# Four chunks of seven block products in each feed-forward, with weights relaid in 4 KB rows

## The chip, the cores and the metric

The kernel runs on one core of a Trainium2 chip. The metric is the device time of one execution in microseconds (us). Engines of the core work side by side, each in the order of its own instruction stream: TensorE (PE, with its weight loads shown as PEld), VectorE (DVE), ScalarE (ACT), GpSimd (POOL) and SyncE (SP), which issues the transfers between device memory and the on-chip buffer.

## What is computed

A block of two layers on 256 tokens of width 1024, in fp32. Six stages follow each other, each ending in a residual sum and a layer normalization: a gated feed-forward, a hybrid mixer (a gated delta rule beside a state-space scan), a feed-forward, a feed-forward, an attention mixer (NSA), a feed-forward. A feed-forward is

```
def swiglu(x, w_in, w_out):
    gate, up = jnp.split(x @ w_in, 2, axis=-1)
    return (jax.nn.silu(gate) * up) @ w_out
```

with `w_in` of 1024 x 5632 and `w_out` of 2816 x 1024. After each stage comes `layer_norm(x * alpha + 0.5 * y)` for a feed-forward, without the 0.5 for a mixer.

## The kernel before

**Precision.** A product of fp32 numbers is made of three faster products. Each operand is split into a high part (rounded to the type fp32r) and a low part (the rest), and the kernel adds high x high, high x low and low x high. `split` (L646) does it: a copy that rounds, on ACT or DVE (on ACT alone while `self.hard` is set, as in a feed-forward), and a subtraction, always on DVE. Weights are split on the chip too: a raw tile arrives by transfer, then `whi` and `wlo` are made of it (`unit`, L655). One such pair of 128 x 1024 costs one ACT and one DVE instruction.

**Feed-forward** (`ffn`, L1046). The 2816 inner columns are 22 tiles of 128, 11 steps of 256. The first two steps (NT) are done with the tokens as the stationary operand (`proj_tok`), then come ordinary steps with the weights stationary (`proj_two`, L867: eight matmuls of 512 columns and eight of 256 for each tile of 128 columns), each followed by gating on ACT and DVE. Four steps' worth of columns go another way: two *chunks* of 512 columns (`wide`, L745). There the 256 tokens and the 1024 inputs are cut in halves, gate and up weights are the two halves of the columns, and the 2 x 2 block product is made of seven block products in place of eight (in the manner of Strassen and Winograd), from sums and differences of blocks. The weight sums are made on DVE, 8 additions of 128 x 1024 a chunk (`add`), then split; the token sums once per stage (`token_forms`, L728). A product is twelve matmuls of 512 columns. The result has tokens on partitions and is transposed by eight 128 x 128 transposes. `WIDE` (L51) says in which half-steps the chunks' parts are issued between the ordinary ones.

**Output.** Each of the 22 inner tiles is one term of the second product: twelve matmuls into four accumulators (`out_mm`, L1063). The last few terms of the second token block are held back (`LAG`, 5) until the first block's normalization has begun.

**Order.** The program is first written down as a list; `Plan.order` (L344) then simulates the engines with a cost for each instruction and writes down a fixed order for each engine's stream. Buffers are 36 tiles of 128 x 1024 (`m4`) with quotas by purpose, four raw tiles of 128 x 2048 and two tiles for x. A load is issued by SP when its raw tile is free. POOL does little in a feed-forward but one power for each normalization (`lnve`).

All instructions have line L546 in the profile, since they are issued there; they are told apart by tile names.

Of the kernel before, what the change touches and what calls it, by code (L numbers as in the profile page):

```python
# [18 lines left out]
P = 128  # L19
# [7 lines left out]
RAW, M4 = 4, 36  # L27

CAPS = {
    "raw": (RAW, "SB"), "m4": (M4, "SB"), "x": (2, "SB"),  # L30
# [4 lines left out]
QUOTAS = {"M": None, "D": None, "F": None, "S": (8, 8), "Z": (4, 4), "L": (4, 4), "G": (6, 6), "P": (5, 5), "Q": (5, 5), "W": (12, 24)}  # L35

KEPT = ("L", "G", "F")
# [13 lines left out]
WIDE = ("", "ab", "cd", "ef", "g", "ab", "cd", "ef", "g", "")  # L51
# [4 lines left out]
KEEP_WARM = 5500  # L56

# [121 lines left out]
class Plan:  # L179
# [81 lines left out]
    def price(self, op, eng, fn, args, kw):  # L261
# [15 lines left out]
        if fn == "dma_start":  # L277
            return 60.0
# [65 lines left out]
    def order(self, caps):  # L344
# [25 lines left out]
        dma_free = 0.0  # L370
# [69 lines left out]
        while left:  # L440
# [58 lines left out]
            if fn == "dma_start":  # L499

                dma_free = max(dma_free, st + 1300) + op.nbytes / (290.0 if st < 8000.0 else 360.0)
                op.end = dma_free + 600
                free[e] = st + c
            else:
                op.end = st + c
                free[e] = st + c
# [63 lines left out]
class K:  # L570
    NT = 2
    LAG = 5
# [82 lines left out]
    def unit(self, srcs, parts):  # L655

        raw = self.plan.tile("raw", [P, 2048], F32, "raw", stream="W")
        for dst, src in srcs:
            self.nc.sync.dma_start(dst(raw), src)
        out = []  # L660
        for f in parts:
            v = f(raw)
            n = int(v.ids.size)
            shape = v.shape
            hi = self.m4(n, "whi", "W", F32R)
            lo = self.m4(n, "wlo", "W", F32R)
            if len(shape) == 3:
                hi, lo = (t.rearrange("p (a b) -> p a b", a=shape[1]) for t in (hi, lo))
            self.split(hi, lo, v)
            out.append((hi, lo))  # L670
        return out

    def unit_cols(self, w, c0, n):

        v3 = lambda r: r[:, :KD * n].rearrange("p (k n) -> p k n", k=KD)
        parts = [lambda r, e=e: v3(r)[:, :, e * P:(e + 1) * P] for e in range(n // P)]
        return self.unit([(v3, w[:, :, c0:c0 + n])], parts)

    def unit_rows(self, w, k0, nk, c0, n):

        v3 = lambda r: r[:, :nk * n].rearrange("p (k n) -> p k n", k=nk)
        g = min(nk, 1024 // n)
        out = self.unit([(v3, w[:, k0:k0 + nk, c0:c0 + n])],
                        [lambda r, e=e: v3(r)[:, e:e + g, :] for e in range(0, nk, g)])
        return [(hi[:, k, :], lo[:, k, :]) for hi, lo in out for k in range(g)]

    def tok_weights(self, w, c0, n):

        nk = 2048 // n
        out = []  # L690
        for k0 in range(0, KD, nk):
            out += self.unit_rows(w, k0, min(nk, KD), c0, n)
        return out

    def pair_weights(self, w, c0, c1, n):

        out = []
        for k0 in range(0, KD, 4):
            raw = self.plan.tile("raw", [P, 2048], F32, "raw", stream="W")
            for g, c in enumerate((c0, c1)):  # L700
                dst = raw[:, g * 1024:g * 1024 + 4 * n]
                self.nc.sync.dma_start(dst.rearrange("p (k n) -> p k n", k=4), w[:, k0:k0 + 4, c:c + n])
            v = raw.rearrange("p (g k n) -> p k g n", g=2, k=4)
            for e in range(0, 4, 2):
                hi, lo = self.m4(1024, "whi", "W", F32R), self.m4(1024, "wlo", "W", F32R)
                self.split(*(t.rearrange("p (k g n) -> p k g n", k=2, g=2) for t in (hi, lo)), v[:, e:e + 2])
                hi, lo = (t.rearrange("p (k c) -> p k c", k=2) for t in (hi, lo))
                out += [(hi[:, k, :], lo[:, k, :]) for k in range(2)]
        return out

    def first_weights(self, w, c0, arrivals):

        out = []
        for k0 in range(0, KD, 2):
            if k0 % 4 == 0:
                raw = self.plan.tile("raw", [P, 2048], F32, "raw", stream="W")
            v = H3(raw[:, k0 % 4 * 512:(k0 % 4 + 2) * 512], 2)
            hi, lo = (H3(self.m4(1024, n, "W", F32R), 2) for n in ("whi", "wlo"))
            step = 1 if arrivals and k0 < 4 else 2
            for e in range(0, 2, step):  # L720
                self.nc.sync.dma_start(v[:, e:e + step], w[:, k0 + e:k0 + e + step, c0:c0 + 512])
                self.split(hi[:, e:e + step], lo[:, e:e + step], v[:, e:e + step])
                for f in (arrivals.pop(0) if arrivals else []):
                    f()
            out += [(hi[:, k, :], lo[:, k, :]) for k in range(2)]
        return out

    def token_forms(self, x):  # L728

        V = self.nc.vector  # L730
        (a11, a21), (a12, a22) = ((X[:, 0], X[:, 1]) for X in x[3])
# [5 lines left out]
        for X in x[3]:  # L737
            hi, lo = (self.m4(1024, n, "F", F32R).rearrange("p (b k t) -> p b k t", b=2, k=4) for n in ("fhi", "flo"))
            self.split(*(t.rearrange("p b k t -> p (b k t)") for t in (hi, lo, X)))
            out += [(hi[:, b], lo[:, b]) for b in range(2)]  # L740
        s2, s3, s4, s1 = out
        part = lambda b, k0: tuple(x[e][:, k0:k0 + 4, b, :] for e in range(2))
        return dict(a=part(0, 0), b=s1, c=part(0, 4), d=s2, e=s3, f=part(1, 4), g=s4)

    def wide(self, w_in, c0, forms, gout, then):  # L745

        nc, V = self.nc, self.nc.vector
        h4 = lambda t: H3(t, 4)

        def load(k0, c):  # L750
            raw = self.plan.tile("raw", [P, 2048], F32, "raw", stream="W")
            nc.sync.dma_start(h4(raw), w_in[:, k0:k0 + 4, c:c + 512])
            return raw

        def halves(src):
            out = []
            for e in range(2):
                hi, lo = self.m4(1024, "whi", "W", F32R), self.m4(1024, "wlo", "W", F32R)
                self.split(hi, lo, src[:, e * 1024:e * 1024 + 1024])
                out.append((H3(hi, 2), H3(lo, 2)))  # L760
            return out

        def add(out, a, b):
            for e in range(2):
                cs = slice(e * 1024, e * 1024 + 1024)
                V.tensor_tensor(out[:, cs], a[:, cs], b[:, cs], OP.add)

        def product(bank, name, w, start):
            ah, al = forms[name]

            def mm(*args, start=False, stop=False, on={} if start else dict(skip_group_check=True)):
                nc.tensor.matmul(*args, start=start, stop=stop, **on)
            for e, (wh, wl) in enumerate(w):
                for k in range(2):
                    n = 2 * e + k
                    mm(bank, ah[:, n], wh[:, k], start=start and n == 0)
                    mm(bank, al[:, n], wh[:, k])
                for k in range(2):
                    n = 2 * e + k
                    mm(bank, ah[:, n], wl[:, k], stop=n == 3)  # L780

        b11 = load(0, c0)
        w = halves(b11)
        b12 = load(0, DFF + c0)
        p, q = self.bank("mp"), self.bank("mp")
        s, u, v, sg = (H3(self.m4(1024, n, "F"), 2)[:, e] for n in ("su", "vg") for e in range(2))
        product(p, "a", w, True)
        nc.scalar.activation(s, p, AF.Copy)
        yield
        add(b11, b11, b12)  # L790
        product(q, "b", halves(b11), True)
        yield
        b21 = load(4, c0)
        product(p, "c", halves(b21), False)
        nc.scalar.activation(sg, p, AF.Silu)
        yield
        b22 = load(4, DFF + c0)
        add(b11, b11, b22)
        product(p, "d", halves(b11), True)
        V.tensor_tensor(u, p, s, OP.add)  # L800
        yield
        add(b12, b12, b22)
        product(p, "e", halves(b12), False)
        V.tensor_tensor(v, p, s, OP.add)
        V.tensor_tensor(v, q, v, OP.subtract)
        yield
        add(b11, b11, b21)
        product(p, "f", halves(b11), False)
        V.tensor_tensor(s, p, s, OP.add)
        nc.scalar.activation(s, s, AF.Silu)  # L810
        yield
        product(q, "g", halves(b22), False)
        V.tensor_tensor(u, q, u, OP.subtract)
        V.tensor_tensor(sg, sg, u, OP.mult)
        V.tensor_tensor(s, s, v, OP.mult)
        gh, gl = gout
        for b, g in enumerate((sg, s)):
# [3 lines left out]
            self.split(gh[:, :, b * P:(b + 1) * P], gl[:, :, b * P:(b + 1) * P], h4(pt))  # L821
        then()
# [10 lines left out]
    def new_x(self, name="x"):  # L833

        t = self.plan.tile("x", [P, KD, 2, 2, P], F32R, "x", stream="")
        return [t[:, :, 0], t[:, :, 1], t]

    def new_forms(self, x):

        x.append([self.m4(1024, f"X{q}", "F").rearrange("p (b k t) -> p b k t", b=2, k=4) for q in range(2)])  # L840
        return x

    def transpose_half(self, x, b, h, q, scale=None, c0=None):
# [7 lines left out]
        if len(x) > 3:  # L851
# [1381 lines left out]
```

## Time and profile before

| | before |
|---|---|
| median of 3 runs | 1104.2 us (1102.8 to 1106.8) |
| the profiled execution | 1103.9 us |
| its span (first to last instruction) | 1102.2 us |
| PE / DVE / ACT / POOL busy | 1082.8 / 939.7 / 653.3 / 45.1 us |
| moved by DMA | 201 MB |
| packets under 2 KB / under 8 KB | 90074 / 132314 |

Busy time is the time in which an engine had an instruction in flight. Matmuls overlap and their ends are modelled, so PE at 98% need not be PE at its peak; the starts of the weight loads tell more. In names, `whi` and `wlo` are the weights' parts, `raw` the weights as they arrive, `x` the tokens' parts, `fhi` and `flo` the parts of the token sums, `g`, `gh`, `gl` the gated tiles, `ps`, `mp`, `acc` accumulators. `su` and `vg` hold a chunk's intermediate results, `sg` an ordinary step's.

### The profile page before, as it was taken

What the parts mean: (1) busy time and instruction counts of PE and PEld (TensorE: products, weight loads), DVE (VectorE), ACT (ScalarE), POOL (GpSimd) and SP (SyncE); (2) the same over time, 40 slices, a digit from 0 to 9 for tenths busy, and PEclk for the clock granted to TensorE, in tenths of its full rate; (3) what the DMA queues carried; (4) which work ended last, traced back from release to release, by engine and by line L of the source; (5) the groups of instructions that cost most, each with busy time, mean ns of one, the idle gap of its engine ahead of it and who ended that gap; (6) DMA issues with size and microseconds to landing.
All of it is one profiled execution on the core that took longest, in us unless ns stands there. A gap on an engine that the chain in (4) does not pass through costs nothing.

```text
span 1102.2 us, 16098 instructions
## 1 busy us (share of the span) xinstructions
PE 1082.8 (98%) x6234; PEld 917.0 (83%) x6234; DVE 939.7 (85%) x1417; ACT 653.3 (59%) x1106; POOL 45.1 (4%) x85
## 2 busy tenths in 40 slices
PE   9999999998999999999999999999999999999997
PEld 6888878897999887888888888888887778888885
DVE  7969879798969999969877988979778979879694
ACT  7647565168736756647464756647356777556460
POOL 1000000002000311000000000000000100000000
PEclk9999999999999999999999999999999999999999
DMA  9628468542825175539369445639526227446361
GB/s 309 236 104 295 147 221 280 191 137 65 243 93 204 68 251 180 202 115 314 106 238 296 162 145 194 209 127 301 181 84 255 77 80 267 151 169 217 118 222 39
DMA packets 132391, 201.01 MB, mean 182 GB/s; under 512 B 9485, under 2 KB 90074, under 8 KB 132314
## 3 DMA queue, kind: packets, MB, share of 16 engines
q1 hardware_dynamic: 132314, 199.97, 53.6%
q8 instruction: 49, 0.80, 0.3%
q14 instruction: 28, 0.23, 0.1%
HBM read 197.18 MB, written 1.07 MB: 180 GB/s over the span
## 4 chain that ended last, share of the span: by engine, by line
PE 57%; DVE 3%; ACT 1%; issue 0%; DVEq 0%
PE ps L546 25%; PE acc L546 19%; PE mp L546 14%; DVE arena L546 1%; DVE h L546 1%; ACT whi L546 1%; DVE wlo L546 0%; DVE P L546 0%; DVE qs L546 0%; DVE x L546 0%; DVE whi L546 0%; DVE vbd L546 0%; DVE lnst L546 0%; DVE kd L546 0%; DVE qT L546 0%
## 5 line engine op out<-in xcount | busy, mean ns | idle before, releaser
L546 DVE TENSOR_TENSOR wlo<-raw,whi 128x1024 fp32r<-128x1024 f32 (+2 forms) x399 | 473.1, 1208 | 58.5 <-ACT whi L546 57.1
L546 ACT ACTIVATE whi<-raw 128x1024 fp32r<-128x1024 f32 (+2 forms) x374 | 374.5, 1045 | 96.0 <-DMA raw<-in_ffn_w_in_dram 47.7
L546 PE MATMUL ps<-x,whi 128*128 128x512 f32 (+2 forms) x1072 | 247.4, 352 | 2.6 <-ACT cv L546 2.2
L546 PEld LDWEIGHTS ps<-x,whi 128*128 128x128 f32 (+1 forms) x1072 | 185.4, 189 | 28.1 <-ACT cv L546 3.5
L546 PE MATMUL ps<-x,wlo 128*128 128x256 f32 x856 | 153.2, 284 | 0.0
L546 PE MATMUL acc<-whi,g 128*128 128x512 f32 x444 | 145.8, 390 | 0.0
L546 PEld LDWEIGHTS ps<-x,wlo 128*128 128x128 f32 x856 | 129.1, 190 | 6.5
L546 PE MATMUL ps<-whi,x 128*128 128x512 f32 (+1 forms) x480 | 129.4, 386 | 0.9 <-ACT x L546 0.5
L546 PEld LDWEIGHTS ps<-whi,x 128*128 128x128 f32 x480 | 85.7, 188 | 17.0 <-issue 1.1
L546 PEld LDWEIGHTS acc<-whi,g 128*128 128x128 f32 x444 | 83.5, 188 | 16.7
L546 PE MATMUL acc<-wlo,g 128*128 128x512 f32 x222 | 86.9, 391 | 0.0
L546 ACT ACTIVATE sg<-ps 128x256 f32<-128x256 f32 x92 | 34.8, 379 | 70.3 <-PE ps L546 69.8
L546 DVE TENSOR_TENSOR raw<-raw,raw 128x1024 f32<-128x1024 f32 x64 | 75.8, 1217 | 0.3
L546 PE MATMUL acc<-whi,x 128*128 128x512 f32 x224 | 73.8, 404 | 1.9 <-DVE x L546 1.0
L546 PE MATMUL ps<-wlo,x 128*128 128x512 f32 (+1 forms) x240 | 68.1, 382 | 0.0
L546 DVE TENSOR_TENSOR sg<-ps,sg 128x256 f32<-128x256 f32 (+1 forms) x94 | 39.7, 424 | 17.2 <-ACT sg L546 15.9
L546 PE MATMUL mp<-whi,x 128*128 128x512 f32 x192 | 51.5, 390 | 1.0 <-DVE vg L546 0.6
L546 PE MATMUL mp<-whi,fhi 128*128 128x512 f32 x128 | 50.3, 393 | 0.8 <-ACT whi L546 0.5
L546 PEld LDWEIGHTS acc<-whi,x 128*128 128x128 f32 x224 | 41.4, 188 | 11.1 <-ACT whi L546 2.1
L546 PE MATMUL mp<-whi,flo 128*128 128x512 f32 x128 | 49.9, 390 | 0.0
L546 PE MATMUL acc<-whi,gh 128*128 128x512 f32 x127 | 49.7, 391 | 0.0
L546 PE MATMUL acc<-wlo,gh 128*128 128x512 f32 x127 | 49.7, 391 | 0.0
(287 smaller groups left out, 1575.7 us busy)
## 6 DMA issues: line engine op xcount, KB each, us to landing
raw<-in_ffn_w_in_dram SPq DMA_DIRECT2D x72, 1024.0 KB, 5.2
raw<-in_ffn_w_out_dram SPq DMA_DIRECT2D x44, 1024.0 KB, 5.0
raw<-in_hyb_w_in_dram SPq DMA_DIRECT2D x20, 1024.0 KB, 5.2
raw<-in_ffn_w_in_dram SPq DMA_DIRECT2D x30, 512.0 KB, 5.0
raw<-in_hyb_w_out_dram SPq DMA_DIRECT2D x8, 1024.0 KB, 5.0
raw<-in_nsa_w_in_dram SPq DMA_DIRECT2D x5, 1024.0 KB, 5.6
raw<-in_nsa_cmp_w_dram SPq DMA_DIRECT2D x4, 1024.0 KB, 5.3
raw<-in_nsa_w_out_dram SPq DMA_DIRECT2D x4, 1024.0 KB, 6.5
```

The source lines that it names most:

```text
L546: r = getattr(getattr(nc, eng), fn)(*[res(a) for a in args], **{k: res(a) for k, a in kw.items()})
```

## The change

- **Four chunks** in each feed-forward (`CHUNKS`), so that one ordinary step is left of five. They come one after the other behind the ordinary step, and `TERMS` says how many output terms follow each part of a chunk. The seven products are in another order and use one bank of `ps` for a running sum, so that five in place of seven 512-wide DVE operations combine them, and three ACT copies in place of one.
- **Weights relaid on the host** (`laid_out`, a change of order only): each 128 x 1024 tile is contiguous, 4 KB a partition, and arrives in one transfer of 512 KB. Raw tiles come out of the common pool, now of 52 tiles; so do those of x, four for the high and low parts of 256 inputs each. Splitting a transposed half of x takes two instructions of 256 elements in place of one of 512, on each of the two engines.
- **Seven output row tiles** (`ADDED`: 8, 10, ... 20) get their low part without DVE: ACT writes the negated, rounded copy of the weights, a transfer issued by POOL adds the weights from device memory to it, and ACT makes the high part.
- Output weights are asked for three terms ahead (`AHEAD`); `LAG` is 7. The planner gets a price for transfers that POOL issues and another model of the DMA rate.

```diff
-RAW, M4 = 4, 36
+M4 = 52
-WIDE = ("", "ab", "cd", "ef", "g", "ab", "cd", "ef", "g", "")
+CHUNKS, AHEAD, LAG = 4, 3, 7
+TERMS = ((0, 1, 1, 1, 1, 1, 1), (0, 0, 1, 1, 1, 1, 0), (0, 0, 1, 1, 1, 1, 0), (0, 0, 1, 1, 1, 0, 0))
+ADDED = range(8, 22, 2)
...
+    def arrive(self, src, name="raw"):
+        n = int(np.prod(src.shape[1:]))
+        raw = self.m4(n, name, "W")
+        self.nc.sync.dma_start(raw, src)
+        return raw
...
+    def rows(self, w, f, added=False):
+        nc = self.nc
+        raw = self.arrive(w[f])
+        if not added:
+            return self.halved(raw)
+        hi, lo = self.m4(1024, "whi", "W", F32R), self.m4(1024, "wlo", "W", F32R)
+        nc.scalar.activation(lo, raw, AF.Copy, scale=-1.0)
+        nc.gpsimd.dma_start(lo, w[f], accum_op=OP.add)
+        nc.scalar.activation(hi, raw, AF.Copy)
+        return hi, lo
...
     def wide(...):
+        r, q = self.bank("ps"), self.bank("mp")
+        b11 = load(0)
+        product(r, "a", b11, True, False)
+        nc.scalar.activation(s, r, AF.Copy)
         yield
+        b12 = load(1)
+        add(b11, b12)
+        product(q, "b", b11, True, False)
         yield
+        b22 = load(2)
+        add(b11, b22)
+        product(r, "d", b11, False, False)
+        nc.scalar.activation(t, r, AF.Copy)
         yield
+        add(b12, b22)
+        product(r, "e", b12, False, False)
+        nc.scalar.activation(v, r, AF.Copy)
         V.tensor_tensor(v, q, v, OP.subtract)
         yield
+        product(q, "g", b22, False, True)
+        V.tensor_tensor(u, q, t, OP.subtract)
+        yield
+        b21 = load(3)
+        p = self.bank("ps")
+        product(p, "c", b21, True, True)
         V.tensor_tensor(s, p, s, OP.add)
         nc.scalar.activation(s, s, AF.Silu)
+        V.tensor_tensor(u, s, u, OP.mult)
         yield
+        add(b11, b21)
+        product(r, "f", b11, False, True)
+        nc.scalar.activation(t, r, AF.Silu)
+        V.tensor_tensor(v, t, v, OP.mult)
...
     def ffn(...):
+        def weights_to(n):
+            while len(wos) < min(n, NF):
+                wos.append(self.rows(w_out, len(wos), len(wos) in ADDED))
+
+        def flush(most):
+            for f, g in [terms.pop(0) for _ in range(min(most, len(terms)))]:
+                weights_to(f + AHEAD)
+                out_mm(0, f, g, wos[f])
...
+        weights_to(AHEAD)
+        for n in range(CHUNKS):
+            f0 = 2 * steps + 4 * n
+            part = self.wide(w_in, 8 + 4 * (steps - NT) + 8 * n, forms, gout)
+            for most in TERMS[n]:
+                next(part)
+                flush(most)
+            terms.extend((f0 + e, tuple(t[:, e, :] for t in gout)) for e in range(4))
+        flush(NF)
```

More of the change, by code (lines that the diff above doesn't have):

```diff
@@ L499, in order @@
             if fn == "dma_start":
-                dma_free = max(dma_free, st + 1300) + op.nbytes / (290.0 if st < 8000.0 else 360.0)
-                op.end = dma_free + 600
+                at, need = st + 1300, op.nbytes * (2 if e == "gpsimd" else 1)
+                while need > 0:
+                    n = int(at / 500)
+                    room = (155e3 if at < 8000.0 else 190e3) - moved.get(n, 0)
+                    take = min(need, room, room * (n + 1 - at / 500), 95e3 if e == "gpsimd" else need)
+                    moved[n] = moved.get(n, 0) + take
+                    need -= take
+                    at = (n + 1) * 500.0 if need > 0 else max(at, n * 500.0 + 500.0 * moved[n] / 190e3)
+                op.end = at + 600
                 free[e] = st + c
@@ new lines, in halved, with tiled @@
+    def halved(self, raw):
+        n = int(raw.ids.size)
+        hi, lo = self.m4(n, "whi", "W", F32R), self.m4(n, "wlo", "W", F32R)
+        if HARD:
+            self.nc.scalar.activation(hi, raw, AF.Copy)
+            self.nc.vector.tensor_tensor(lo, raw, hi.bitcast(F32), OP.subtract)
+        else:
+            self.split(hi, lo, raw)
+        return hi, lo
+    def tiled(self, srcs, k):
+        out = []
+        for src in srcs:
+            hi, lo = self.halved(self.arrive(src))
+            n = int(hi.ids.size) // k
+            hi, lo = (t.rearrange("p (k n) -> p k n", n=n) for t in (hi, lo))
@@ L687, in tok_weights @@
-    def tok_weights(self, w, c0, n):
-        nk = 2048 // n
-        out = []
[L691 to L722, printed above, removed]
+    def col_tiles(self, srcs):
+        return self.tiled(srcs, KD)
@@ new lines, in first_weights @@
+    def first_weights(self, w, n0, arrivals):
+        out = []
+        for n in range(4):
+            src = w[n0 + n]
+            raw = self.m4(1024, "raw", "W")
+            hi, lo = (self.m4(1024, name, "W", F32R) for name in ("whi", "wlo"))
+            step = 512 if arrivals and n < 2 else 1024
+            for e in range(0, 1024, step):
+                cs = slice(e, e + step)
+                self.nc.sync.dma_start(raw[:, cs], src[:, cs])
+                self.split(hi[:, cs], lo[:, cs], raw[:, cs])
@@ L743, in token_forms, with wide @@
         return dict(a=part(0, 0), b=s1, c=part(0, 4), d=s2, e=s3, f=part(1, 4), g=s4)
-    def wide(self, w_in, c0, forms, gout, then):
+    def wide(self, w, n0, forms, gout):
         nc, V = self.nc, self.nc.vector
[L748 to L756, printed above, removed]
-            for e in range(2):
[L758 to L763, printed above, removed]
-            for e in range(2):
[L765 to L773, printed above, removed]
@@ new lines, in load, with add, product @@
+        def load(block):
+            return [self.arrive(w[n0 + 2 * block + e]) for e in range(2)]
+        def add(out, a):
+            for e in range(2):
+                V.tensor_tensor(out[e], out[e], a[e], OP.add)
+        def product(bank, name, src, start, stop):
+            ah, al = forms[name]
+            on = {} if start and stop else dict(skip_group_check=True)
+            mm = nc.tensor.matmul
+            for e in range(2):
+                wh, wl = (H3(t, 2) for t in self.halved(src[e]))
@@ L783, in wide @@
[L783 to L788, printed above, removed]
+                    mm(bank, ah[n], wl[:, k], start=False, stop=n == 3, **on)
+        r, q = self.bank("ps"), self.bank("mp")
+        s, t, u, v = (H3(self.m4(1024, n, "F"), 2)[:, e] for n in ("su", "vg") for e in range(2))
@@ L996, in go @@
             self.mm3(acc[b][c], st(b), (w[0][:, cs], w[1][:, cs]), first and f == 0, last and f == n - 1)
-        cut = max(0, n - self.LAG) if last else n
+        cut = max(0, n - LAG) if last else n
         for f in range(cut):
@@ L1077, in ffn @@
             for s in range(NT):
-                steps.append(self.pair_weights(w_in, s * 256, DFF + s * 256, 256))
+                steps.append(self.row_tiles([w_in[4 * s + n] for n in range(4)], 2))
             for b in range(2):
@@ L1093, in ffn @@
                 self.scale_h(b)
-        todo = []
-        late = []
-        def flush(keep, most=NF):
-            while len(todo) > keep and most:
-                most -= 1
-                f, g, wo = todo.pop(0)
-                out_mm(0, f, g, wo)
-                if count[0, 0] > NF - self.LAG - (3 if last else 0):
-                    late.append((f, g, wo))
-                else:
-                    out_mm(1, f, g, wo)
-        steps = NF // 2 - 2 * sum("a" in turn for turn in WIDE)
@@ new lines, in weights_to @@
+        def weights_to(n):
[5 more added lines that the diff above has]
+                out_mm(0, f, g, wos[f])
+                if count[0, 0] > NF - LAG - (3 if last else 0):
+                    late.append((f, g, wos[f]))
+                else:
+                    out_mm(1, f, g, wos[f])
@@ L1707, in out_a @@
             for s in range(4):
-                wo = self.unit_rows(w_out, 2 * s, 2, 0, D)
+                wo = [self.rows(w_out, 2 * s + e) for e in range(2)]
                 for e in range(2):
@@ L1718, in hybrid @@
         for s in range(4):
[L1719 removed]
+            wo = [self.rows(w_out, 8 + 2 * s + e) for e in range(2)]
             terms += [((lambda b, k=2 * s + e: self.xb(oT[1], b, k)), wo[e]) for e in range(2)]
@@ L1918, in dense @@
                 yield
-            yield from queries(1, self.tok_weights(w_in, 512, 512), range(2))
+            yield from queries(1, self.row_tiles([w_in[4 + n] for n in range(4)], 2), range(2))
         kcb = self.sm([P, 2, 2, 16], "kcb")
```

277 lines of the change are left out of this document (118 added, 159 removed).

## The prediction, as written before the result

> **What bounds the kernel now.** I read the page's busy times first, then busy time by stage, then TensorE's weight loads one by one, then what VectorE spends in a feed-forward stage. PE is busy for 98% of the span, DVE for 85%:
>
> ```profile
> span 1102.2 us, 16098 instructions
> PE 1082.8 (98%) x6234; PEld 917.0 (83%) x6234; DVE 939.7 (85%) x1417; ACT 653.3 (59%) x1106; POOL 45.1 (4%) x85
> ```
>
> The stretches below are, in order, feed-forward 1, the hybrid mixer, feed-forward 2 and 3, the NSA mixer, feed-forward 4, cut at the end of each stage's second normalization. Columns after the length: busy us (instructions) of PE, PEld, DVE, ACT, POOL, then granted clock, DMA share, GB/s. The clock is 0.99 to 1.00 everywhere, so nothing here is a throttle.
>
> ```profile
> 0.00:199.50 199.50, 194.16 (x931) 159.84 (x932) 165.39 (x207) 119.93 (x171) 5.48 (x22) 1.00 0.66 223
> 199.50:436.00 236.50, 231.66 (x1855) 207.65 (x1854) 210.47 (x409) 144.00 (x261) 24.74 (x33) 0.99 0.50 161
> 436.00:618.00 182.00, 182.00 (x898) 153.74 (x896) 156.34 (x193) 108.08 (x151) 1.85 (x2) 1.00 0.59 202
> 618.00:798.00 180.00, 180.00 (x910) 153.28 (x909) 154.52 (x210) 103.55 (x151) 3.00 (x4) 1.00 0.58 194
> 798.00:921.00 123.00, 121.64 (x788) 95.88 (x788) 106.98 (x216) 85.44 (x243) 8.06 (x23) 1.00 0.40 141
> 921.00:1102.20 181.20, 173.33 (x863) 146.60 (x861) 146.02 (x187) 92.35 (x132) 1.97 (x3) 0.99 0.46 161
> ```
>
> Matmul busy time can flatter, so the check is the pitch of the weight loads: does the next one start when the last matmul's columns are through? This is a view of PE's weight loads in order of time, in feed-forward 2 (start, us, what, count), plus two rows from the end of a chunk:
>
> ```profile
> 468.04 1.77 PEld L546 LDWEIGHTS ps<-x,whi 128*128 128x128 f32 x8
> 469.85 1.13 PEld L546 LDWEIGHTS ps<-x,wlo 128*128 128x128 f32 x8
> 470.91 1.70 PEld L546 LDWEIGHTS ps<-x,whi 128*128 128x128 f32 x8
> 472.64 1.13 PEld L546 LDWEIGHTS ps<-x,wlo 128*128 128x128 f32 x8
> 473.70 0.19 PEld L546 LDWEIGHTS acc<-whi,g 128*128 128x128 f32 x1
> ...
> 476.34 0.87 PEld L546 LDWEIGHTS mp<-whi,x 128*128 128x128 f32 x4
> 477.25 0.41 PEld L546 LDWEIGHTS mp<-wlo,x 128*128 128x128 f32 x2
> 477.70 0.87 PEld L546 LDWEIGHTS mp<-whi,x 128*128 128x128 f32 x4
> 478.61 0.41 PEld L546 LDWEIGHTS mp<-wlo,x 128*128 128x128 f32 x2
> 479.06 0.19 PEld L546 LDWEIGHTS mp<-whi,fhi 128*128 128x128 f32 x1
> ...
> 587.44 0.57 PEld L546 LDWEIGHTS mp<-ident,su 128*128 128x128 f32 x4
> ...
> 588.25 0.45 PEld L546 LDWEIGHTS mp<-ident,vg 128*128 128x128 f32 x4
> 588.66 1.24 PEld L546 LDWEIGHTS ps<-x,whi 128*128 128x128 f32 x6
> ```
>
> Eight 512-column matmuls take 1.77 to 1.81 us, 0.226 each, and there is no hole in the rows. So the feed-forward stages are bound by PE's issue, and less PE work there is less time as long as DVE follows. Three prices are read here: two ordinary 128-column tiles 473.70 - 468.04 = 5.66 us; one block product of twelve matmuls 479.06 - 476.34 = 2.72 us; an output term of twelve matmuls 476.34 - 473.70 = 2.64 us. The eight transposes of a chunk take 1.2 to 1.3 us (587.44 to 588.66, with one foreign load between).
>
> **The change on PE.** A chunk replaces two ordinary steps of 256 columns. Two steps are eight tiles, 8/2 x 5.66 = 22.64 us. A chunk is 7 x 2.72 = 19.04 plus 1.3 for transposes, 20.3 us. That is 2.3 us less per chunk; two more chunks in each of four stages make 8 x 2.3 = 18.4 us less PE time. The order of the seven products and their banks changes, not their number.
>
> **The change on DVE.** Here are the groups of the stretch 436 to 618 by shape, and DVE in order of time for the pitch of one instruction when they are back to back:
>
> ```profile
> L546 DVE TENSOR_TENSOR wlo<-raw,whi 128x1024 fp32r<-128x1024 f32 x81 | 96.8, 1218 | 15.9 <-ACT whi L546 15.7
> L546 ACT ACTIVATE whi<-raw 128x1024 fp32r<-128x1024 f32 x78 | 78.4, 1053 | 21.3 <-DMA raw<-in_ffn_w_in_dram 14.3 <-DMA raw<-in_ffn_w_out_dram 3.8 <-DVE raw L546 2.2
> L546 DVE TENSOR_TENSOR raw<-raw,raw 128x1024 f32<-128x1024 f32 x16 | 19.1, 1218 | 0.0
> L546 ACT ACTIVATE sg<-ps 128x256 f32<-128x256 f32 x25 | 9.4, 378 | 16.6 <-PE ps L546 16.6
> L546 ACT ACTIVATE su<-mp 128x512 f32<-128x512 f32 x2 | 1.2, 591 | 2.3 <-PE mp L546 2.3
> L546 DVE SCALAR_TENSOR_TENSOR h<-acc,h 128x512 f32<-128x512 f32 x4 | 2.7, 687 | 5.7 <-PE acc L546 5.7
> ...
> 439.60 0.68 DVE L546 TENSOR_TENSOR x<-mp,x 128x512 fp32r<-128x512 f32 x1
> 440.20 1.22 DVE L546 TENSOR_TENSOR wlo<-raw,whi 128x1024 fp32r<-128x1024 f32 x1
> 441.33 0.42 DVE L546 TENSOR_TENSOR sg<-ps,sg 128x256 f32<-128x256 f32 x1
> 441.67 2.35 DVE L546 TENSOR_TENSOR wlo<-raw,whi 128x1024 fp32r<-128x1024 f32 x2
> ```
>
> The pitches are 1.13 us at 1024 elements (440.20 to 441.33), 0.60 at 512 (439.60 to 440.20), 0.34 at 256 (441.33 to 441.67). Per stage, two more chunks need 28 low parts instead of 16 for the same weights, +12 x 1.13 = 13.6; 16 more block additions, +18.1; seven 512-wide operations each, +8.4. The four ordinary steps they replace had eight 256-wide ones each, -32 x 0.34 = -10.9. The two chunks that were there lose two 512-wide operations each, -2.4. Seven output tiles give their low part away, -7.9. Together +18.9 us per stage: 156.3 becomes 175.2 in a stage that PE would do in 182 - 4.6 = 177.4. So DVE goes from 86% to 99% of the stage. That is the crux.
>
> Where that load lies: a chunk with four output terms costs PE 20.3 + 4 x 2.64 = 30.9 us. DVE has in it 14 low parts, 8 additions, 7 small operations and two output low parts (the other two are among the seven): 24 x 1.13 + 4.2 = 31.3. The second and third chunk are a tie. The fourth has three terms, PE 28.2 against DVE's 31.3. The first has six, PE 36.1 against 27 x 1.13 + 4.2 = 34.7. So DVE falls up to 0.4 + 0.4 + 3.1 = 3.9 us behind, less what it is ahead by when the chunks begin. The pool allows 28 weight tiles, about two products ahead (5 us). The lead would cover all of it if nothing else used it, but the waits of an in-order engine use it too. I take 1.6 us of stall per stage, two fifths of the 3.9; over four stages **+6.4**. The ends are 0 (the lead covers it) and, from the rivals below, more than the 18.4 gained.
>
> **The low parts by transfer.** ACT gains 12 high parts and 7 negating copies at 1.05 (20.0), 2 x 7 operations of 512 at about 0.6 and four more in the old chunks (10.8), and loses 32 of 256 at about 0.38 (12.2): 108 becomes 127 of 177 us, so it costs nothing while ACT keeps a quarter idle. No row of before has a transfer issued by POOL, let alone one that adds, so its price is bounded by these landing times:
>
> ```profile
> raw<-in_ffn_w_out_dram SPq DMA_DIRECT2D x44, 1024.0 KB, 5.0
> raw<-in_hyb_w_in_dram SPq DMA_DIRECT2D x4, 512.0 KB, 3.8
> DMA to landing us min/median/max: 3.6/5.2/11.1
> ```
>
> Below, 3.8 us (512 KB); above, 11.1 (the slowest weight load). Before it stand the plain load (at most 5.0) and the copy (1.05), and the tile is asked for three output terms ahead. With a product between two terms that is 3 x (2.64 + 2.72) = 16.1 us of cover. At 11.1 the chain is 17.2, late by 1.1; at the median landing, 5.2, it is 11.3 and hidden. I take the median: the size alone would say 3.8, but it shares the DMA engines with the loads. Hence **0**. [...]
>
> On POOL the transfer's issue waits for ACT's copy. Behind it stands only the normalization's power (rows of lnve), which comes after the last of the seven; nothing else in the stage uses POOL.
>
> **Rows and loads.** The queue that issues loads waits mostly for buffers:
>
> ```profile
> SPq L546 <- DVE wlo L546: 564.2, 127, 26.0
> ```
>
> With transfers of 512 KB in place of 1 MB its issues about double; it waits for VectorE's low parts for 564 us now, and that slack covers them. DMA is at 0.40 to 0.66 by stage. PE's rows have no hole for lack of data in feed-forward 2, so 4 KB rows win **0** there; the ends are -5.3 (all of PE's idle time in feed-forward 1, 199.5 - 194.2, where the first loads are waited for) and +1. The seven transfers read 3.7 MB per stage a second time, beside 202 GB/s x 182 us = 36.8 MB, 10% more traffic on a DMA that is 59% busy. The split of x in halves makes one 0.60 operation into two of 0.34: 0.07 more each, four per boundary, with the first half 0.27 sooner: ends +1.4 and -1.4 over five boundaries, taken as **0**. The mixers get another order of the same work; they leave PE 4.8 and 1.4 us idle, the most that can be won there, and I take 0.
>
> **Sum**, against the profiled execution (1103.9 us, 1.7 outside its 1102.2 span): 1102.2 - 18.4 + 6.4 + 1.7 = 1091.9. The median of the runs shown, 1104.2, is 0.3 above that execution: **1092**. Its own range is 1087 to 1099.
>
> **Rivals.** *The whole PE gain arrives.* DVE's lead covers the fourth chunk: 1104.2 - 18.4 = 1086, down to 1081 with the early idle time. For it, DVE already is full in stretches like this one, and PE is unbroken in them:
>
> ```profile
> 440.00:450.00 10.00, 10.00 (x48) 8.20 (x47) 10.00 (x13) 6.92 (x11) 0.00 (x0) 1.00 0.84 299
> ```
>
> Against it, 99% of a stage leaves 2 us for every wait.
>
> *DVE takes the stage.* The wait moves from PE's issue to low parts. Of 182 us DVE now idles 25.7, of it 15.7 waiting for high parts and 5.7 for the accumulators, as the rows above show. 182 - 175.2 = 6.8 us of that may stay without the stage getting longer than before. If so much stays, a quarter, the gain is gone: 1104; if half stays (12.9), each stage is 6 us longer and the kernel ends at 1128. For it: in-order DVE, three engines in a row per tile. Against: much of this idle time was there because nothing was urgent.
>
> *The adding transfer is late.* The place is the eighth to the twentieth output tile, 28 of them; PE waits in order for each low part. At 1.1 us each that is 31 us, 1086 + 31 = 1117, slower. It decides from 18.4/28 = 0.66 us late per tile, that is a landing above 16.1 + 0.66 - 6.05 = 10.7 us. For it: two queues share the 16 DMA engines, and the slowest load took 11.1; against: the median is 5.2.
>
> *The saving isn't one*: the new chunk's products run slower than the old ones'. Nothing in the rows speaks for it, since the instructions are the same; left at nothing.
>
> **How the numbers follow.** Within 0.3% (3.3 us) counts as no change. Forecast 42%, whole gain 24%, DVE takes the stage 19% (1 faster, 10 no change, 8 slower), late transfer 15% (2 no change, 13 slower): faster 67%, same 12%, slower 21%. Range 1081 to 1112: the lower end is the whole gain with the early idle time; the upper stops short of the late transfer and of half the idle time staying.
>
> **What would show it.** Right: PE's instructions in the feed-forwards fall by about 70 each, products stay at 2.72 us, DVE is above 95% of feed-forward 2 and 3, these take 179 and 177 us, PE's waits there name wlo from DVE. Wrong: PE waiting for wlo from a DMA (late transfer); DVE full and stages of 180 us or more (DVE takes the stage); stages of 177 and no wait (whole gain); or a change in the mixers' 236.5 and 123 us by more than 4 us, which my sum has at zero.

## The result, and the profile after

| | before | after |
|---|---|---|
| median | 1105.5 us (1102.8 to 1107.7) | 1087.3 us (1087.2 to 1087.4) |
| ratio | | 0.984, interval 0.982 to 0.986 |
| profiled execution / its span | 1103.9 / 1102.2 us | 1087.2 / 1085.5 us |

One of the four executions of the changed kernel took 2747.9 us, for a reason that is not known, and stands in none of these numbers. The kernel became 1.6% faster, 18.2 us by the medians and 16.7 us between the two profiled executions. The page of the changed kernel begins so:

```profile
span 1085.5 us, 16212 instructions
PE 1066.3 (98%) x5946; PEld 893.3 (82%) x5946; DVE 1010.9 (93%) x1453; ACT 725.9 (67%) x1155; POOL 70.7 (7%) x116
```

PE has 288 matmuls fewer, 72 per feed-forward (about 70 were forecast), DVE is 71 us busier and ACT 73 us.

Here are the six stages of the changed kernel, cut at PE's last accumulating matmul of each stage (the prediction cut them a few microseconds later, at the second normalization). Columns after the length: busy us (instructions) of PE, PEld, DVE, ACT, POOL, then granted clock, DMA share, GB/s.

```profile
0.00:186.80 186.80, 181.88 (x831) 149.17 (x832) 175.42 (x199) 136.03 (x177) 10.67 (x28) 1.00 0.75 247
186.80:423.60 236.80, 232.34 (x1858) 206.79 (x1857) 213.84 (x429) 147.12 (x272) 26.20 (x33) 1.00 0.49 164
423.60:599.20 175.60, 175.60 (x818) 145.75 (x817) 172.52 (x196) 123.02 (x159) 8.01 (x9) 1.00 0.68 221
599.20:774.80 175.60, 175.60 (x818) 146.05 (x817) 171.81 (x214) 120.18 (x159) 9.17 (x11) 1.00 0.66 220
774.80:902.70 127.90, 125.48 (x811) 99.83 (x810) 107.69 (x224) 87.81 (x251) 7.65 (x25) 0.97 0.45 150
902.70:1085.50 182.80, 175.36 (x820) 145.70 (x818) 169.67 (x197) 111.78 (x143) 8.96 (x10) 0.99 0.59 186
```

In feed-forward 2 and 3 DVE is busy for 98% of the time, and yet PE is busy for all of it. NSA is the stage with a granted clock below 0.99. The same cut applied to all kernels gives this table, the map for all that follows. Each cell is the stage's length, and behind the sign what PE stood idle plus what it lost by clock ((1 - granted clock) x length, summed over 120 slices of the stage), in us:

| kernel | FF 1 | hybrid | FF 2 | FF 3 | NSA | FF 4 | four FFs | two mixers |
|---|---|---|---|---|---|---|---|---|
| before | 193.1 / 5.3+0 | 235.6 / 4.0+1.7 | 182.0 / 0.9+0 | 180.3 / 0+0 | 123.4 / 1.4+0 | 187.8 / 7.9+2.3 | 743.2 | 359.0 |
| after | 186.8 / 4.9+0 | 236.8 / 4.5+0 | 175.6 / 0+0 | 175.6 / 0+0 | 127.9 / 2.4+3.4 | 182.8 / 7.4+2.4 | 720.8 | 364.7 |

So the feed-forwards gained 22.4 us and the mixers, of which the change touches the order alone, gave 5.7 back: hybrid 1.2, NSA 4.5. 22.4 - 5.7 is the 16.7 between the profiled executions.

**Feed-forward.** The groups of feed-forward 2 by shape, answering the prediction's (last columns: busy, mean ns | idle just before, and what ended it):

```profile
L561 DVE TENSOR_TENSOR wlo<-raw,whi 128x1024 fp32r<-128x1024 f32 x85 | 100.3, 1218 | 1.1 <-ACT whi L561 0.6
L561 ACT ACTIVATE whi<-raw 128x1024 fp32r<-128x1024 f32 x90 | 91.0, 1059 | 25.0 <-DVE raw L561 23.8 <-PE acc L561 0.6 <-DMA raw<-in_ffn_w_in_dram 0.2
L561 DVE TENSOR_TENSOR raw<-raw,raw 128x1024 f32<-128x1024 f32 x32 | 38.3, 1217 | 0.0
```

DVE used to idle 15.9 us here before its low parts, waiting for ACT's high parts; now 1.1 us are left. ACT in its turn waits 23.8 us for DVE's sums. The two have changed places, and DVE now carries the stage beside PE without a hole.

PE's weight loads in the same stage (start, us, what, count): one block product from its first load to the first load of the output term behind it, then the two groups of four transposes of a chunk, each with the load that follows it.

```profile
472.13 0.19 PEld L561 LDWEIGHTS ps<-whi,fhi 128*128 128x128 f32 x1
...
474.85 0.19 PEld L561 LDWEIGHTS acc<-whi,g 128*128 128x128 f32 x1
...
491.19 0.59 PEld L561 LDWEIGHTS mp<-ident,vg 128*128 128x128 f32 x4
491.75 0.19 PEld L561 LDWEIGHTS acc<-whi,g 128*128 128x128 f32 x1
...
494.40 0.58 PEld L561 LDWEIGHTS mp<-ident,vg 128*128 128x128 f32 x4
494.96 0.77 PEld L561 LDWEIGHTS ps<-whi,x 128*128 128x128 f32 x4
```

A product is 474.85 - 472.13 = 2.72 us as before. Eight transposes are 0.56 + 0.56 = 1.12 us (491.75 - 491.19 and 494.96 - 494.40), where 1.3 was put down.

**The adding transfer.** The page's issues, and the view of the tile `wlo` on POOL (duration of the issue min/median/max in ns, first and last start; then issue to landing):

```profile
raw<-in_ffn_w_out_dram SPq DMA_DIRECT2D x88, 512.0 KB, 3.7
wlo<-in_ffn_w_out_dram POOLq DMA_DIRECT2D x28, 512.0 KB, 8.5
```

```profile
L561 POOL DMA_DIRECT2D wlo<-in_ffn_w_out_dram x28: 844/862/1046, 88.2 to 1053.5; - x28
...
DMA to landing us min/median/max: 5.4/8.5/11.2
```

An adding transfer of 512 KB lands after 8.5 us by the median, a plain one of the same size from the same tensor after 3.7. PE has no wait for `wlo` from a DMA anywhere in the run: the transfers were in time.

**NSA.** Windows of the changed kernel around the place where the clock falls (columns as above):

```profile
840.00:846.00 6.00, 6.00 (x47) 5.13 (x43) 6.00 (x16) 5.88 (x18) 1.22 (x5) 1.00 0.35 124
846.00:849.00 3.00, 1.11 (x7) 0.64 (x6) 2.97 (x10) 2.96 (x11) 0.28 (x1) 0.94 0.49 158
849.00:855.00 6.00, 5.53 (x24) 5.23 (x25) 5.71 (x11) 5.47 (x21) 0.00 (x0) 0.50 0.00 1
855.00:858.00 3.00, 3.00 (x18) 2.01 (x19) 2.34 (x8) 1.40 (x7) 0.00 (x0) 0.92 0.00 0
```

PE stands idle for 1.9 us out of three, in pieces none of which is longer than 0.83 us (waits for DVE, ACT and POOL on small tiles of the attention), and then runs at a granted clock of 0.50 for more than six. In the kernel before the same work, at 860 to 866 us, had 1.1 us of idle time in six and kept its clock; that row is from its windows:

```profile
860.00:866.00 6.00, 4.92 (x37) 4.03 (x37) 6.00 (x16) 6.00 (x22) 2.82 (x6) 1.00 0.54 178
```

### The profile page after: what moved, and what is told of

Read it like the earlier page. It is cut to its first block, busy times and chain, and to the rows that moved or that the text cites. A ratio compares the mean times of both kernels' runs of the same rounds, so it can differ in the third digit from the quotient of the medians.

```text
span 1085.5 us, 16212 instructions
## 1 busy us (share of the span) xinstructions
PE 1066.3 (98%) x5946; PEld 893.3 (82%) x5946; DVE 1010.9 (93%) x1453; ACT 725.9 (67%) x1155; POOL 70.7 (7%) x116
## 4 chain that ended last, share of the span: by engine, by line
PE 84%; DVE 12%; ACT 1%; DMA 1%; issue 1%; POOL 0%; SPq 0%; DVEq 0%; ACTq 0%
PE ps L561 39%; PE acc L561 31%; PE mp L561 14%; DVE wlo L561 2%; DVE cv L561 2%; DVE arena L561 1%; DMA raw<-in_ffn_w_in_dram 1%; DVE o L561 1%; DVE sw L561 1%; DVE x L561 1%; DVE y L561 1%; DVE qs L561 1%; DVE AT L561 0%; POOL arena L561 0%; DVE Y L561 0%
## 5 line engine op out<-in xcount | busy, mean ns | idle before, releaser
L561 ACT ACTIVATE whi<-raw 128x1024 fp32r<-128x1024 f32 (+1 forms) x435 | 436.8, 1052 | 104.0 <-DVE raw L561 85.4
L561 PE MATMUL ps<-whi,x 128*128 128x512 f32 (+1 forms) x864 | 234.8, 390 | 0.3 <-ACT cv L561 0.3
L561 PEld LDWEIGHTS ps<-whi,x 128*128 128x128 f32 x864 | 156.7, 188 | 30.6 <-issue 1.5
L561 DVE TENSOR_TENSOR raw<-raw,raw 128x1024 f32<-128x1024 f32 x128 | 152.8, 1216 | 0.0
L561 PE MATMUL ps<-x,whi 128*128 128x256 f32 (+2 forms) x560 | 114.3, 312 | 4.0 <-ACT cv L561 2.4
L561 PEld LDWEIGHTS ps<-x,whi 128*128 128x128 f32 (+1 forms) x560 | 90.4, 188 | 11.4 <-ACT cv L561 3.8
L561 PE MATMUL acc<-whi,gl 128*128 128x512 f32 x253 | 97.9, 390 | 0.0
L561 PEld LDWEIGHTS ps<-wlo,x 128*128 128x128 f32 x432 | 79.6, 188 | 15.3 <-issue 0.4
L561 PE MATMUL ps<-x,wlo 128*128 128x256 f32 (+1 forms) x344 | 80.0, 284 | 0.5 <-DVE wlo L561 0.5
L561 PE MATMUL acc<-whi,g 128*128 128x512 f32 x192 | 63.3, 392 | 0.0
```

The source lines that it names most:

```text
L561: r = getattr(getattr(nc, eng), fn)(*[res(a) for a in args], **{k: res(a) for k, a in kw.items()})
```

## The experiments

Theories to tell apart. *Feed-forward:* PE's shorter work sets the stages and DVE's load costs nothing as long as it fits; or DVE at 98% already costs something, and the gain would be larger with less on it. *Transfers:* they free DVE for little; or they take DMA time from the loads. *Mixers:* the other order of the parts costs the 5.7 us; or the transfers do, through DMA.

**1. Two chunks, no transfers.** The new layout, pool and halved x with the old amount of block products; an output term follows each tile of an ordinary step.

```diff
-CHUNKS, AHEAD, LAG = 4, 3, 7
+CHUNKS, AHEAD, LAG = 2, 3, 7
-TERMS = ((0, 1, 1, 1, 1, 1, 1), (0, 0, 1, 1, 1, 1, 0), (0, 0, 1, 1, 1, 1, 0), (0, 0, 1, 1, 1, 0, 0))
+TERMS = ((0, 0, 1, 1, 1, 1, 0), (0, 0, 1, 1, 1, 0, 0))
-ADDED = range(8, 22, 2)
+ADDED = ()
...
                 terms.append((f, g))
+                flush(1)
```

> The changed kernel with two chunks and five ordinary steps, as before, and no adding transfers; rows of 4 KB, common pool and halved x stay. Theory (the gain is PE work alone): the feed-forwards come back by 8 x 2.48 = 20 us, so 1104 to 1110, as the kernel before. Rival (rows and pool bring part of the gain): 1095 or less.

Measured: 1113.1 us, ratio 1.007 (1.005 to 1.010), above the range expected, and by the mixers alone. The stages, in their order, from the windows:

```profile
0.00:194.20 194.20, 188.95 (x903) 156.42 (x904) 158.92 (x201) 123.77 (x179) 4.48 (x21) 1.00 0.63 220
194.20:433.90 239.70, 232.19 (x1858) 206.84 (x1857) 214.15 (x427) 145.30 (x268) 27.75 (x33) 1.00 0.48 161
433.90:615.00 181.10, 180.79 (x890) 152.10 (x889) 153.28 (x192) 109.93 (x157) 1.92 (x2) 1.00 0.59 195
615.00:795.90 180.90, 180.60 (x890) 152.21 (x889) 153.60 (x211) 109.28 (x161) 2.95 (x4) 1.00 0.57 193
795.90:924.20 128.30, 125.29 (x811) 99.36 (x810) 107.59 (x224) 87.85 (x251) 7.67 (x25) 0.97 0.45 150
...
```

The four feed-forwards take 743.6 us, before 743.2: layout, pool and halves together bring nothing there. The mixers take 368.0, 9 us more than before, and NSA shows the granted clock of 0.97 again, with no transfer in the kernel. So a loss in the mixers needs neither the transfers nor the additional chunks.

**2. Two chunks with the transfers.** As 1, with `ADDED` as in the change.

> The changed kernel with two chunks, as the run without adding transfers, but with the seven adding transfers. Theory (they matter only where VectorE is full): feed-forwards within 1 us of the run without them, the kernel 1108 to 1115. Rival (they always save time): 1103 or less.

Measured: 1117.4 us, ratio 1.012 (1.010 to 1.014), above the theory's 1115. The feed-forwards take 748.6 in the profiled execution, 5.0 more than without transfers, where 1 was allowed. By the medians of all executions the kernels differ by 4.3 us, and their ranges just touch (1108.7 to 1115.2 without, 1115.1 to 1120.9 with). Where DVE had room (busy for 85% of feed-forward 2 in experiment 1) the transfers brought nothing, and probably cost a little. PE's waits over the whole run, in us, times, longest, first of this kernel and then of the kernel without transfers:

```profile
PE mp L561 <- DVE vg L561: 4.3, 6, 1.4
```

```profile
PE mp L561 <- DVE vg L561: 1.2, 3, 0.7
```

Of the 5.0 us, 3.1 are longer waits for the chunks' gated results. Why these come later with the transfers was not settled.

**3. Four chunks, no transfers.**

```diff
-ADDED = range(8, 22, 2)
+ADDED = ()
```

> The changed kernel with the low parts of all output tiles on VectorE. Theory (VectorE is full, and PE is not late only because the seven low parts left it): 7.9 us more for VectorE in each feed-forward, against 3 to 4 us that it idles there now; feed-forward 2 and 3 get 4 to 5 us longer, 1 and 4 less, so 1096 to 1104, with PE waiting for wlo from VectorE. Rival (enough is prefetched, the transfers save nothing): 1086 to 1090.

Measured: 1102.7 us, ratio 0.998 (0.997 to 0.999), 15.4 us behind the change. Its feed-forward 2 and 3, from the windows:

```profile
432.80:608.60 175.80, 175.80 (x819) 146.03 (x817) 175.49 (x196) 116.50 (x148) 1.91 (x2) 1.00 0.60 205
608.60:787.10 178.50, 176.34 (x810) 144.53 (x809) 177.78 (x218) 114.95 (x152) 2.95 (x4) 1.00 0.57 191
```

DVE is busy for 99.8% of feed-forward 2, and the stage is as long as with the transfers, 175.8, without a hole in PE. Feed-forward 3 is 2.9 us longer, 2.2 of it PE idle: 1.2 and 0.6 us are waits for ACT, which a few microseconds before the longer of them had waited 5.4 us for a sum of DVE. So the time lies in the range expected, but feed-forward 2 did not get longer, and PE's waits are not for `wlo` from DVE. The feed-forwards lose 6.7 us in all (727.5), the rest of the loss is in the mixers: hybrid 243.5 (+6.7), NSA 130.0 (+2.1). That made the mixers' order the next thing to look at.

**4. Fourteen transfers in a row.** All of the last fourteen row tiles of the output weights.

```diff
-ADDED = range(8, 22, 2)
+ADDED = range(8, 22)
```

> The changed kernel with 14 output tiles (8 to 21) by the adding transfer in place of 7. Theory (transfers land in time, and PE bounds the stage): 1086 to 1090 with VectorE some 8 us less busy in each feed-forward. Rival (the transfer is close to late; two in flight land later): PE waits for wlo or the accumulators' terms, 1095 or more.

Measured: 1123.1 us, ratio 1.018 (1.016 to 1.020): 36 us behind the change and in the rival's range. Experiment 6 shows more of it.

**5. Three transfers** in place of seven.

```diff
-ADDED = range(8, 22, 2)
+ADDED = range(8, 14, 2)
```

> The changed kernel with three adding transfers (tiles 8, 10, 12) in each feed-forward, four low parts more for VectorE, 4.5 us a stage, against 3 to 4 us that it idles. Theory (VectorE's idle time is the margin, beyond it the lateness moves into the stage behind): between 1088 and 1096. Rival (each moved low part counts in full, whatever the margin): 4/7 of the 15.4 us between 0 and 7, so 1096.

Measured: 1093.8 us, ratio 0.990 (0.989 to 0.992). The feed-forwards take 720.1, as with seven (720.8). The loss of 6.5 us is in the hybrid mixer (244.0 against 236.8), most of it at one hole; its windows, and the wait at that place:

```profile
381.00:384.00 3.00, 0.74 (x4) 0.31 (x3) 3.00 (x11) 0.00 (x0) 0.00 (x0) 0.93 0.01 3
384.00:391.00 7.00, 6.63 (x22) 5.32 (x22) 6.44 (x14) 6.26 (x14) 1.51 (x1) 0.54 0.52 150
391.00:394.00 3.00, 3.00 (x15) 2.17 (x13) 1.99 (x3) 2.27 (x3) 1.08 (x1) 1.00 0.48 160
```

```profile
PE mp L561 <- DVE y L561: 2.3, 1, 2.3
```

PE waits 2.3 us once, for a result of DVE, and nearly seven microseconds at half clock follow (0.54 in that row), 3.4 us more. The time lies in the range of the theory, but whether DVE's lateness or the mixer's order made the hole, this run doesn't tell; experiment 9 does.

**6. Seven transfers in a row at the stage's end**, the same number as the change has.

```diff
-ADDED = range(8, 22, 2)
+ADDED = range(15, 22)
```

> The changed kernel with the seven adding transfers for tiles 15 to 21 in a row. Theory (it was not the number of 14 transfers that cost 36 us but the DMA, full at the end of the stage, so that the next stage's weights and VectorE behind them were late): most of the loss with half the transfers, 1105 or more, a hole in PE at a stage's start with half clock behind it. Rival (the number counts): 1095 or less.

Measured: 1129.3 us, ratio 1.023 (1.021 to 1.024), worse than fourteen. So it is not their number. The end of feed-forward 1, from the windows, and what PE waited for from 150 to 200 us:

```profile
160.00:170.00 10.00, 8.10 (x35) 6.02 (x33) 8.03 (x9) 10.00 (x12) 1.71 (x2) 1.00 1.05 315
170.00:180.00 10.00, 9.85 (x47) 8.15 (x48) 7.42 (x10) 7.25 (x10) 2.57 (x3) 1.00 1.05 299
180.00:190.00 10.00, 9.80 (x44) 7.78 (x42) 4.53 (x7) 3.34 (x4) 0.00 (x0) 1.00 1.04 330
190.00:200.00 10.00, 4.97 (x16) 3.63 (x17) 10.00 (x21) 4.20 (x8) 1.09 (x2) 0.73 0.82 307
```

```profile
PE mp L561 <- DVE h L561: 4.6, 1, 4.6
PE acc L561 <- DMA wlo<-in_ffn_w_out_dram: 2.1, 2, 1.3
```

And DVE in order of time at that place, with what ended its wait:

```profile
182.35 0.69 DVE L561 CAST whi<-raw 128x1024 fp32r<-128x1024 f32 x1
188.48 1.29 DVE L561 SCALAR_TENSOR_TENSOR h<-acc,h 128x512 f32<-128x512 f32 x2 [5.44 <-PE acc L561]
```

The 16 DMA engines are full for 30 us (a share of 1.04 to 1.05 in the first three rows). The adding transfers come late for the last output terms (2.1 us here, 6.7 in the whole run), the residual sum `h` on DVE waits 5.4 us for PE's accumulators, the normalization behind it is late, and PE, with no other work left, waits 4.6 us for it and loses clock, to 0.73 of that stretch. In the changed kernel, where a transfer is issued for every second tile, the DMA is nearly as full for 20 us of it (1.03 and 0.97), but PE has no hole:

```profile
160.00:170.00 10.00, 10.00 (x46) 8.27 (x45) 10.00 (x11) 9.05 (x11) 1.09 (x2) 1.00 1.03 318
170.00:180.00 10.00, 10.00 (x50) 8.37 (x49) 9.04 (x12) 7.34 (x9) 0.00 (x0) 1.00 0.97 336
```

So a full DMA alone didn't make the hole. Whether the row of transfers or their place among the last terms does, these runs don't separate.

With fourteen the first links differ: ACT then waits 9.8 us at one place for the mixer's first weights, `raw<-in_hyb_w_tok_dram`, DVE 1.9 us for the same, and the residual sum 3.4 us. The end is the same wait of PE for `h`; its row in order of time:

```profile
192.75 1.51 PE L561 MATMUL mp<-ident,h 128*128 128x128 f32 x6 [3.93 <-DVE h L561]
```

**7. One-kilobyte rows.** The input weights of the feed-forwards stored as four blocks of 256 columns per tile, so that a row of the transfer is 1 KB in place of 4.

```diff
-        self.nc.sync.dma_start(raw, src)
+        if len(src.shape) == 3:
+            self.nc.sync.dma_start(raw.rearrange("p (j n) -> p j n", j=4), src)
+        else:
+            self.nc.sync.dma_start(raw, src)
...
-    a['ffn_w_in'] = np.stack(ffn)
+    a['ffn_w_in'] = np.ascontiguousarray(np.stack(ffn).reshape(4, -1, P, 4, 256).transpose(0, 1, 3, 2, 4))
```

> The changed kernel with the rows of the feed-forwards' first weights at 1 KB in place of 4 KB, same tiles and same order of work. Theory (no matmul waits for weights, the rows are hidden): 1086 to 1090, landing times up to some us longer. Rival (the rows carry part of the gain): 1093 or more.

Measured: 1090.6 us, ratio 0.988 (0.986 to 0.989), 3.3 us behind the change, between the ranges of theory and rival. All of it is feed-forward 1 (190.1 against 186.8). The first 14 us, of this kernel and then of the changed one:

```profile
0.00:14.00 14.00, 9.96 (x29) 6.43 (x30) 3.95 (x11) 5.31 (x11) 3.49 (x20) 0.88 0.88 277
```

```profile
0.00:14.00 14.00, 10.67 (x40) 7.08 (x41) 5.89 (x15) 7.35 (x17) 3.47 (x20) 1.00 0.83 295
```

Median landing goes from 5.5 to 6.1 us. That showed only at the kernel's start, where nothing is loaded ahead; 1.7 of the 3.3 us are clock lost there. Later stages take the same time within 0.7 us.

**8. Another order in NSA.** `weave` takes the next piece of work from the part that is least far by cost over share; these are the shares of NSA's four parts.

```diff
-W_NSA = (70.0, 60.0, 40.0, 20.0)
+W_NSA = (57.0, 66.0, 87.0, 14.0)
```

> The changed kernel with other shares for the four strands of the NSA mixer (57, 66, 87, 14), so another order of the same instructions there. Theory (the mixer is 4.5 us longer after the change because PE has a hole of 1.4 us that is followed by 7 us at half the granted clock, an accident of the order): without a hole of that size the clock stays at 1.00, the mixer takes 123 to 125 in place of 128 us, the kernel 1082 to 1085. Rival (the small transfers, the pool or the halved x cost it): 127 us or more again, 1086 to 1090.

Measured: 1083.3 us, ratio 0.981 (0.980 to 0.982). NSA takes 123.5 us, before 123.4, and its clock stays whole; the windows of the same work:

```profile
838.00:845.00 7.00, 7.00 (x46) 6.02 (x44) 6.84 (x11) 7.00 (x17) 0.07 (x1) 1.00 0.54 155
845.00:852.00 7.00, 6.42 (x44) 4.35 (x42) 6.97 (x14) 6.17 (x24) 2.68 (x5) 1.00 0.44 147
852.00:859.00 7.00, 6.82 (x57) 5.01 (x56) 6.71 (x18) 2.69 (x9) 0.00 (x0) 1.00 0.46 151
```

The feed-forwards take 721.5, so the whole difference of 4 us is the mixer. What the change lost in NSA was one hole and the clock behind it, and it comes back by order alone.

**9. Three transfers and another order in both mixers.** As 5, with `W_HYB = (59, 123, 30, 38, 12)` and `W_NSA = (71, 70, 94, 15)`.

> Three adding transfers, and other shares for the strands of both mixers (hybrid 59, 123, 30, 38, 12; NSA 71, 70, 94, 15). The run with three alone lost 8 us to the changed kernel, but its four feed-forwards took 720 us in sum against 721; the hybrid mixer took 244 against 237. Theory (that loss is the order of the mixer, a hole in PE before its output with half clock behind it, and not VectorE): hybrid 235 to 238, NSA 122 to 125, the kernel 1079 to 1085. Rival (VectorE's lateness is carried into the mixer): hybrid 242 or more, 1088 or more.

Measured: 1083.1 us, ratio 0.981 (0.979 to 0.983). This and experiment 8 are the best two and can't be told apart; both beat the changed kernel by some 4 us. Its hybrid mixer, feed-forward 2 and NSA:

```profile
186.20:423.40 237.20, 232.79 (x1866) 207.44 (x1865) 213.62 (x429) 148.59 (x279) 24.92 (x33) 1.00 0.51 165
423.40:599.20 175.80, 175.80 (x818) 145.97 (x817) 174.84 (x196) 119.25 (x154) 4.55 (x5) 1.00 0.64 214
774.70:898.30 123.60, 123.02 (x811) 97.19 (x810) 107.17 (x220) 89.75 (x257) 8.60 (x26) 1.00 0.48 158
```

The hybrid mixer is back at 237.2 with DVE as full as in experiment 5, so its hole there was a matter of order. DVE is at 99.5% of feed-forward 2, and PE has no hole. Three transfers per stage are enough.

**10. No transfers and another order in both mixers.** As 3, with `W_HYB = (83, 170, 31, 26, 12)` and `W_NSA = (53, 52, 92, 14)`.

> No adding transfers, and other shares for the strands of both mixers (hybrid 83, 170, 31, 26, 12; NSA 53, 52, 92, 14). Theory (of the 15 us that the run without transfers lost, 7 are VectorE's load in the feed-forwards, the rest the mixers' order): feed-forwards 727 us in sum as there, mixers 360 to 363, the kernel 1088 to 1093. Rival (the lateness reaches the mixers): mixers 368 or more, 1096 or more.

Measured: 1092.2 us, ratio 0.989 (0.987 to 0.991), 9.1 us behind experiment 9. The feed-forwards take 726.0 against 720.2: 5.8 us is what the low parts by transfer are worth there (feed-forward 1 2.5, 3 2.8, 4 0.8, 2 nothing). The mixers take 364.9 against 360.8, more than the theory's 360 to 363 and less than the rival's 368: in this kernel the order could be mended only in part, and it stays open how much of those 4.1 us belongs to the missing transfers.

## Why the prediction was right, and where it was not

The forecast was 1092, the result is 1087.3: inside the forecast's own range of 1087 to 1099, though at its lower edge, and nearest to the rival in which the whole PE gain arrives (1086). Of the signs it named, that rival's came: feed-forward 2 and 3 take 175.6 us each and PE waits for nothing, where 179 and 177 and waits for `wlo` from DVE were forecast. The agreement is better than the working and in part luck, since two steps failed with opposite signs: 1091.9 - 1.4 (more saved) - 1.8 (idle time) - 6.4 (no stall) + 5.7 (mixers) = 1088.0, 0.8 above the profiled execution.

**PE's saving** was put at 18.4 us. The price of a product held to the last digit (2.72). The transposes were put at 1.3 us a chunk and are 1.12, so a chunk is 7 x 2.72 + 1.12 = 20.16 us and saves 2.48, eight of them 19.8. Less idle time of PE in feed-forward 1, 2 and 4 (0.4 + 0.9 + 0.5, from the table) brings it to 21.6 of the 22.4 measured; experiment 1 shows that none of this comes from the layout alone.

**DVE's load** was put at 175.2 us per stage and is 172.5 and 171.8 in feed-forward 2 and 3. The count of low parts was 81 + 12 - 7 = 86 and is 85; ACT's 90 high parts are as forecast.

**The stall is the step that failed.** It was taken at 1.6 us per stage, 6.4 in all, because DVE would fall 3.9 us behind towards the last chunk and a part of the lead would be used up by its waits. It measured 0: PE idles 0.0 us in feed-forward 2 and 3. The waits that were to use up the lead went away when DVE became the busier engine (15.9 us before its low parts became 1.1), and ACT waits in its place. Experiments 3 and 9 sharpen it: with DVE at 99.5% and even 99.8% of feed-forward 2, PE did not idle there. In feed-forward 3 of experiment 3, at 99.6% and behind a stage as full, it did, 2.2 us; whether that is lateness carried over or the stage's own load was not separated. The lower end that the prediction gave for this term, that the lead covers it all, is what happened.

**The mixers were the second failure**, put at 0 with "the most that can be won there" as the only thought given to them. They cost 5.7 us. NSA moved by 4.5, over the 4 us that the prediction named as a sign of a wrong sum. What is seen there, a short hole (1.9 us of three) and then half clock (0.50 for some 6.8 us), appears in no step of it. That nothing was a throttle, as it says, was read from rounded rows: the kernel before already lost 1.7 us of clock in the hybrid mixer (see the table of all stages). Experiment 1 shows that such a loss needs neither the transfers nor the new chunks, and experiment 8 removes it in NSA by order alone: its profiled execution takes 1083.0 us, where 1103.9 - 22.4 = 1081.5 would be the feed-forwards' gain with nothing lost elsewhere. For the hybrid mixer's 1.2 us no run tells its cause.

**The adding transfer** was put at 0 and cost nothing visible where it stands, but its landing was taken at 5.2 us and is 8.5. By the prediction's chain, 6.05 + 8.5 = 14.6 of 16.1 us of cover; the point from which it would have decided, 10.7 us, lies below its slowest, 11.2. Experiments 4 and 6 don't test that point: they lose 36 and 42 us with landings hardly longer (median 8.7 in both, slowest 12.6 and 11.9). What fell short there is probably the cover. The prediction's 16.1 us needs a product between two terms, and the kernel's last five terms come one behind the other (`flush(NF)`), with half the work for the last seven (`LAG`). That this is the reason is argued, no run isolates it; in the changed kernel two of the seven transfers belong to these terms and were in time. The loss also goes through a longer chain than the rival had: not 1.1 us per tile, but the end of a stage coming late. All 28 issues on POOL took 844 to 1046 ns, with DVE busy for 98% of feed-forward 2 and 3, in the groups above by subtractions and sums. What makes their landings differ, from 5.4 to 11.2 us, no run here shows.

**DVE takes the stage**, the rival with 1104 or 1128, fell: its idle time did not stay when its work became urgent, the argument that stood against it.

**4 KB rows** were put at 0 between -5.3 and +1. Against 1 KB rows in the same kernel they are worth 3.3 us at the start (experiment 7). Against the kernel before, nothing of that can be read off, since experiment 1 has the 4 KB rows and a feed-forward 1 of 194.2 against 193.1.

## What to carry to other kernels

Two engines that are both at 98% of a stage need not cost each other anything, as feed-forward 2 and 3 show, where each has buffers ahead of the other; so ask what its waits were for before charging a busy engine with stalls. Work taken off an engine that is not yet the bound brought nothing and perhaps cost something (experiment 2, 1117.4 us against 1113.1), and seven transfers in its place did better spread out (1087.3 us) than in a row at the end of a stage (1129.3). After any change to an order, look through the stages that were *not* changed for holes of PE and for the granted clock: here the repair of one of them added more than a fifth to the gain.

## What the hardware did that was not expected

**Half the clock behind a short hole.** In the windows of NSA above PE was idle for 1.9 us of three, in pieces of at most 0.83 us, and the granted clock then stood at 0.50 for about 6.8 us, a loss of 3.4 us on top of the hole. The same after 2.3 us in experiment 5, again a loss of 3.4 us. With 1.1 us of idle time in six (the kernel before) the clock stayed at 1.00. But the size of the hole did not decide it. The same wait of 2.3 us at the same place of the hybrid mixer stands in experiment 1, and its clock stayed whole:

```profile
388.00:391.00 3.00, 0.49 (x2) 0.30 (x2) 3.00 (x10) 0.22 (x1) 0.00 (x0) 1.00 0.16 19
391.00:398.00 7.00, 6.59 (x32) 5.09 (x33) 6.56 (x14) 6.59 (x15) 2.59 (x1) 1.00 0.64 206
```

In experiment 6 even a wait of 3.5 us for an adding transfer, at 773 us, left it whole (1.00 from 775 to 785 us), while at the start of experiment 8 pieces that make up 1.4 us, from 4.7 to 7.8 us, were followed by some 3.4 us at half clock (0.52, 0.50 and 0.89 in the next three stretches of 1.6 us). The measurement gives no threshold: a hole of this size cost nothing more in one run and 3.4 us more in another, and what decides between them no run here shows.

**An adding transfer took more than twice as long as a plain one in the changed kernel**, 8.5 against 3.7 us median for 512 KB (7.2 against 4.4 in experiment 2, 8.7 against 3.6 in experiment 6), and its issue kept POOL busy for 0.86 us. The adding ones are all issued by POOL and the plain ones by SP, so no run tells the adding from the queue.
